# Hybrid decoder layer: small mixer steps later in TensorE's order, and w_out's block sums made from staged weights

## The chip, the cores and the metric

The kernel runs on one core of a Trainium2 chip. The metric is the device time of one execution in microseconds (us), as the median of several runs. The engines are named as in the profile: PE is TensorE (matmuls), DVE is VectorE, ACT is ScalarE, POOL is GpSimd and SP is SyncE, which here only issues DMAs. Each engine works through its own list of instructions in the order in which the program leaves it; between engines there are semaphores.

## The reference

One layer of a hybrid decoder, for a prompt of 2048 tokens and 8 x 4 decode tokens, 1024 channels, all in float32:

```python
proj = rms_norm(x, g_mix_norm) @ w_in          # 256 pool + 512 rnn + 512 gate branch + 256 query
o_pool = pool_mixer(...)                       # causal means over 2/4/8/16 tokens
xc = causal_dwconv(x_rnn, 4 taps)              # then two block-diagonal gates r and i
h  = rg_lru(xc, ...)                           # a = exp(c*r); h_t = a_t*h_(t-1) + sqrt(1-a_t^2)*i_t*xc_t
o_rnn = gelu(g_rnn) * h
o_xa = cross_attn(q, mk, mv)                   # 4 heads into 256 memory tokens
mix = concat(group_rms(o_pool), group_rms(o_rnn), group_rms(o_xa)) * g_mix_out
x = x + mix @ w_out
x = x + (gelu(dwconv(xn @ w_ff_gate)) * (xn @ w_ff_up)) @ w_ff_down
y = rms_norm(x, g_final)
```

It returns y, the new states of pooling, convolutions and recurrence, and the keys and values of the memory.

## The kernel before

Activations are kept with channels on the 128 partitions and tokens along the free axis. The tokens are cut in six column steps s = 0 to 5 of 344 or 348 columns, two to a block. A float32 operand of a matmul is split in a high and a low part (names h and l: ACT makes h by a copy, DVE makes l = x - h), and a product is three matmuls, hh, lh and hl.

Sweep 1 (up to about 250 us) is the recurrent mixer. For each step PE makes four projections: pr{s}0 and pr{s}1 (the recurrence's input) and pq{s}0 and pq{s}1 (the gelu branch), 48 matmuls each. Woven between them are PE's small steps: str (the sums of squares of the next step's x, one column per token tile), bcr (its reciprocal root broadcast over the partitions), sto and bco (the same for the mixer's output), and pg, four pairs of gate matmuls whose input is the convolved xc. Around them a loop runs through the other engines: DVE scales pr into xr and convolves it into xc (`L537`, six scalar_tensor_tensor at `L549` per half), PE makes pg, ACT r and i (`L471`), xc and r (`L482`, `L486`), a (`L488`) and a square root (`L490`), DVE i, the scan (`L491`, `L574`), g (`L591`), and then, in DVE's order, the squares of the next step (`L359`, `L349`), xr and the convolution of the next step. pr and pq share two PSUM buffers.

Where the small steps come in PE's order is set by the class Weave: each small step is a generator, each k step of a projection ticks a clock by its cost, and a generator is resumed once the clock has passed its due time. The due times are the table W.

```python
        yield 0.0, W["norm"] if s else W["norm_0"]
        yield from g_stat(l, 0, tj, J, rsx[:, s, :], name, W["stat"] if s else W["stat_0"])
```

Then come the memory's keys and values and sweep 2 (about 265 to 447 us): pooling, queries, cross-attention (pS scores, softmax on ACT and DVE, pT, pV), written to DRAM as mixp and mixr. Then w_out for block 0: eight outputs po00 to po07, each over eight k tiles of mix. The mix tiles (sm, split in ahm and alm) and the weight tiles (st_wo, split in h_wo and l_wo) go through one ring of three staging buffers, tag "stg":

```python
        st = wp.tile([P, 1024], F32, tag="stg", bufs=3, name="st_" + name)
```

The loads are issued by SP, whose order is that of the program and not a scheduler's; a load waits until the last reader of its buffer is done, and everything behind it on SP waits too. The other engines' order in the sweeps is set by a scheduler; behind them it is that of the program.

The rest (520 to 2120 us) multiplies blocks of 2 x 2 in seven products instead of eight. w_out for the other blocks comes first (the out stage). The class Pair loads four quarters wr11, wr12, wr21, wr22 of a weight pair, makes four sums s1 to s4 of them on DVE the first time (`L1036`), keeps s1 to s4 in DRAM for the following blocks, and makes the operands wt from them (`L1047`, `L1051`).

Of the kernel before, what the change touches and what calls it, by code (L numbers as in the profile page):

```python
# [43 lines left out]
def hybrid_kernel(ctx: ExitStack, tc: tile.TileContext, I, O):  # L44
# [12 lines left out]
    W = dict(pool_0=12.8, attn_0=1.42, soft0_0=9.0, st_p0=18.9, st_x5=13.5,  # L57
             norm_0=9.35, stat_0=2.55, prep_m=2.07, kv=11.0, gate=8.2, norm=14.0, stat=8.5, prep_r=9.7, mix_r=10.2,
             sq_r=1.6, st_r=22.5, mix_5=14.0, sq_5=1.4, st_5=7.0, bc_p=1.0, attn=0.42, soft0=8.5,
# [69 lines left out]

    def w_place(ring, shape, name, dtype):  # L130

        return wp.tile(shape, dtype, tag="w" + ring, bufs=8, name=name)

    def g_load_w(w, src, name, ring, parts=1):
        st = wp.tile([P, 1024], F32, tag="stg", bufs=3, name="st_" + name)
        w += [w_place(ring, [P, 1024], z + name, F32R) for z in ("h_", "l_")]
        for i in range(parts):
            c = slice(i * 1024 // parts, (i + 1) * 1024 // parts)
            nc.sync.dma_start(out=st[:, c], in_=src[:, c])
            split(w[0][:, c], w[1][:, c], st[:, c])  # L140
            yield
# [48 lines left out]
    xhl = [dr.tile([P, 2, 8, n], F32, name=f"xhl{s}") for s, n in enumerate(NCOL)]  # L190

# [172 lines left out]
    def g_norm(x, s, name):  # L364

        n = NCOL[s]
        tj, J = TOK[s]
        l = squares(x, n, name)
        yield 0.0, W["norm"] if s else W["norm_0"]
        yield from g_stat(l, 0, tj, J, rsx[:, s, :], name, W["stat"] if s else W["stat_0"])  # L370
        RB[s] = new_rb(name)
        yield from g_bcast(rsx[:, s, :], n, tj, J, RB[s][:, 0:n], name)
# [491 lines left out]
    wo = [load_w(I["w_out"][0], "wo00", "a")]  # L864
    mix = [load_mix(0, k, n) for k in range(KD)]
    wo += [load_w(I["w_out"][d], f"wo0{d}", "a") for d in range(1, 4)]
# [40 lines left out]
    def short(name, n):  # L907
# [6 lines left out]
          for nm, m in (("gate", 12), ("up", 12), ("down", 12), ("out", 4))}  # L914
# [82 lines left out]
    SEEN = set()  # L997

    class Pair:
# [7 lines left out]
        def load(self, first=False):  # L1007

            nm, q = self.nm, self.q
            self.a, self.sg, self.w = {}, {}, {}  # L1010
            for i, x in ((1, 2), (2, 1), (2, 2), (1, 1)) if first else ((2, 1), (2, 2), (1, 1), (1, 2)):
                if not self.make and (i, x) == (2, 1):
                    continue
                r = v4(f2.tile([P, 512], F32, tag="wr", bufs=NRAW, name=f"wr{i}{x}{self.name}"))
                if nm == "down":
                    g, j = q
                    z = I["w_down"][8 * g + 4 * x - 4:8 * g + 4 * x, :, 256 * j + 128 * i - 128:256 * j + 128 * i]
                    nc.sync.dma_start(out=r, in_=z.rearrange("k p c -> p k c"))
                else:
                    nc.sync.dma_start(out=r, in_=v4(I["w_" + nm][2 * q + i - 1][:, 512 * x - 512:512 * x]))  # L1020
                self.a[i, x] = r
# [19 lines left out]
        def form(self, i):  # L1041
            a, sg = self.a, self.sg
            return (a[1, 1], sg.get(2), sg.get(1), sg.get(3), a[2, 2], a[1, 2], sg.get(4))[i]
# [391 lines left out]

    def do(what, s):
        early.pop((what, s))()
# [15 lines left out]
    do("sigma1", 0)  # L1453
    B0.hi(2)
    B0.lo(2)
    for s in range(2):
        if s:
            do("sigma1", s)
        do("hi2", s)
        do("lo2", s)  # L1460
    for h in range(2):
        S.activation(out=y7[h], in_=y7[h], func=AF.Square)
        V.tensor_tensor(out=ssum["a0"][:, h], in0=ssum["a0"][:, h], in1=y7[h], op=ALU.add)
    for i in (1, 2, 3):
        for s in range(2):
            if i > 1:
                do(f"sigma{i}", s)
            if i < 3:
                do(f"keep{i}", s)
            if i == 2 and s == 0:  # L1470
                do("hi1", 0)
# [192 lines left out]
```

## Time and profile before

| | us |
|---|---|
| runs | 2121.68, 2122.81, 2124.09 (median 2122.81) |
| the profiled run, and its span | 2121.97, 2120.2 |
| PE busy | 2060.7 |
| DVE busy | 1612.6 |
| ACT busy | 1291.2 |
| POOL busy | 98.3 |

In the profile L12 is a line of the kernel, numbers of buffers are left out of names (po for po00 to po07), `out<-in` names what an instruction writes and reads, and x4 is the number of instructions in a row. PE is busy nearly everywhere, so the profile is read from PE's side: where it waits, what for, and what clock it was granted there.

### The profile page before, as it was taken

What the parts mean: (1) busy time and instruction counts of PE and PEld (TensorE: products, weight loads), DVE (VectorE), ACT (ScalarE), POOL (GpSimd) and SP (SyncE); (2) the same over time, 40 slices, a digit from 0 to 9 for tenths busy, and PEclk for the clock granted to TensorE, in tenths of its full rate; (3) what the DMA queues carried; (4) which work ended last, traced back from release to release, by engine and by line L of the source; (5) the groups of instructions that cost most, each with busy time, mean ns of one, the idle gap of its engine ahead of it and who ended that gap; (6) DMA issues with size and microseconds to landing.
All of it is one profiled execution on the core that took longest, in us unless ns stands there. A gap on an engine that the chain in (4) does not pass through costs nothing.

```text
span 2120.2 us, 35326 instructions
## 1 busy us (share of the span) xinstructions
PE 2060.7 (97%) x12996; PEld 2004.2 (95%) x12996; DVE 1612.6 (76%) x2801; ACT 1291.2 (61%) x2322; POOL 98.3 (5%) x136
## 2 busy tenths in 40 slices
PE   8999899999999999999999999999999999999997
PEld 7888798888899999999999999999999999999997
DVE  8777776874988888889897665668778665668774
ACT  7878834552656656566556665557666665557663
POOL 1111000000000000000000000000000000000001
PEclk9999999999999999999999999999999999999997
DMA  7233494335887656678996555677886554677882
GB/s 275 91 137 133 161 326 142 126 131 196 263 229 233 219 201 217 198 235 243 256 264 213 191 179 178 217 258 216 248 249 192 189 185 165 205 269 219 247 219 78
DMA packets 266892, 434.28 MB, mean 205 GB/s; under 512 B 25792, under 2 KB 124832, under 8 KB 266720
## 3 DMA queue, kind: packets, MB, share of 16 engines
q1 hardware_dynamic: 247248, 372.89, 53.4%
q0 software_dynamic: 18240, 57.63, 10.8%
q8 instruction: 102, 1.67, 0.3%
q10 hardware_dynamic: 1232, 1.51, 0.2%
q14 instruction: 70, 0.57, 0.1%
HBM read 297.69 MB, written 139.96 MB: 206 GB/s over the span
## 4 chain that ended last, share of the span: by engine, by line
PE 83%; DVE 5%; ACT 4%; DMA 4%; issue 3%; POOL 0%; SPq 0%; POOLq 0%; ACTq 0%; DVEq 0%
PE bg L1066 10%; PE bu L1066 10%; PE bd L1066 8%; PE ag L1066 6%; PE cg L1066 6%; PE cu L1066 6%; PE au L1066 6%; PE ad L1066 5%; PE cd L1066 5%; PE pq L234 4%; PE po L234 3%; PE bo L1066 2%; PE pu L234 1%; PE co L1066 1%; DMA wr11d<-in_w_down_dram 1%
## 5 line engine op out<-in xcount | busy, mean ns | idle before, releaser
L1164 DVE SCALAR_TENSOR_TENSOR cv<-gt,pv,cv 128x696 f32<-128x696 f32 (+2 forms) x144 | 133.0, 924 | 35.1 <-ACT cv L1159 35.1
L1180 DVE TENSOR_TENSOR u<-u,cv 128x696 f32<-128x696 f32 (+1 forms) x72 | 63.3, 879 | 62.5 <-ACT cv L1176 62.3
L1226 POOL DMA_DIRECT2D ys<-cd x32 | 34.8, 1121 | 1366.6 <-ACT cd L1095 1235.6
L1066 PE MATMUL bd<-h4s,wt4d 128*128 128x348 f32 (+1 forms) x288 | 72.9, 326 | 4.3 <-DVE cd L1088 4.3
L1066 PE MATMUL ag<-h5s,wt5g 128*128 128x348 f32 (+1 forms) x288 | 74.9, 323 | 0.0
L1066 PE MATMUL cg<-h6s,wt6g 128*128 128x348 f32 (+1 forms) x288 | 74.6, 322 | 0.0
L1066 PE MATMUL cg<-h2s,wt2g 128*128 128x348 f32 (+1 forms) x288 | 74.5, 322 | 0.0
L1066 PE MATMUL bg<-h1s,wt1g 128*128 128x348 f32 (+1 forms) x288 | 74.5, 321 | 0.0
L1066 PE MATMUL bg<-h3s,wt3g 128*128 128x348 f32 (+1 forms) x288 | 74.5, 321 | 0.0
L1066 PE MATMUL cu<-h6s,wt6u 128*128 128x348 f32 (+1 forms) x288 | 74.5, 322 | 0.0
L1066 PE MATMUL bg<-h4s,wt4g 128*128 128x348 f32 (+1 forms) x288 | 74.5, 321 | 0.0
L1066 PE MATMUL ag<-h0s,wt0g 128*128 128x348 f32 (+1 forms) x288 | 74.4, 321 | 0.0
L1066 PE MATMUL au<-h0s,wt0u 128*128 128x348 f32 (+1 forms) x288 | 74.4, 320 | 0.0
L1066 PE MATMUL bu<-h4s,wt4u 128*128 128x348 f32 (+1 forms) x288 | 74.4, 320 | 0.0
L1066 PE MATMUL bu<-h3s,wt3u 128*128 128x348 f32 (+1 forms) x288 | 74.4, 320 | 0.0
L1066 PE MATMUL bu<-h1s,wt1u 128*128 128x348 f32 (+1 forms) x288 | 74.4, 320 | 0.0
L1066 PE MATMUL au<-h5s,wt5u 128*128 128x348 f32 (+1 forms) x288 | 74.3, 321 | 0.0
L1066 PE MATMUL cu<-h2s,wt2u 128*128 128x348 f32 (+1 forms) x288 | 74.3, 321 | 0.0
L1066 PE MATMUL cd<-h6s,wt6d 128*128 128x348 f32 (+1 forms) x288 | 73.5, 327 | 0.0
L1066 PE MATMUL bd<-h3s,wt3d 128*128 128x348 f32 (+1 forms) x288 | 71.9, 321 | 1.6 <-ACT t6d L1084 1.6
L1066 PE MATMUL cd<-h2s,wt2d 128*128 128x348 f32 (+1 forms) x288 | 71.5, 321 | 0.0
L1066 PE MATMUL ad<-h5s,wt5d 128*128 128x348 f32 (+1 forms) x288 | 71.5, 321 | 0.0
(559 smaller groups left out, 7496.0 us busy)
## 6 DMA issues: line engine op xcount, KB each, us to landing
hs<-u SPq DMA_DIRECT2D x24, 696.0 KB, 4.1
ys<-cd POOLq DMA_DIRECT2D x20, 696.0 KB, 10.9
wr22g<-in_w_gate_dram SPq DMA_DIRECT2D x36, 256.0 KB, 4.3
wr11g<-in_w_gate_dram SPq DMA_DIRECT2D x36, 256.0 KB, 4.8
wr12g<-in_w_gate_dram SPq DMA_DIRECT2D x36, 256.0 KB, 5.1
wr22u<-in_w_up_dram SPq DMA_DIRECT2D x36, 256.0 KB, 6.6
wr11u<-in_w_up_dram SPq DMA_DIRECT2D x36, 256.0 KB, 6.5
wr12u<-in_w_up_dram SPq DMA_DIRECT2D x36, 256.0 KB, 6.5
```

Of the source, the lines that this page charges most:

```text
L234: T.matmul(o, w_[:, ks], z, start=(k == 0 and i == 0), stop=(k == nk - 1 and i == 2))
L1066: T.matmul(pt[:, 0:n], w[:, w_, ks_(k)], blk.hl[i][a_][:, k, :], start=(i in (0, 2) and k == m == 0), stop=(k == 3 and m == 2), skip_group ...
L1164: V.scalar_tensor_tensor(out=cv[:, z0:nn], in0=gt[:, z0 + t:nn + t], scalar=pcol("fcw", 3 * f + t), in1=cv[:, z0:nn], op0=ALU.mult, op1=AL ...
L1180: V.tensor_tensor(out=u, in0=u, in1=k["cv"][:, i, 0:nn], op=ALU.mult)
L1226: at[N + 14 + 1 + s].append(lambda j=2 * d + s, k=ks[s]: G.dma_start(out=flat(ys[b][j]), in_=qv(k["c"], n), accum_op=ALU.add, max_dma_last ...
```

## The change

There are two parts.

First, five due times of W become larger, and the first step's norm gets its own (norm_1, stat_1): gates 8.2 to 10.3, norm 14 to 20, st_x5 13.5 to 17, attn 0.42 to 2.5. Only sweep 1 changes in PE's order.

Second, four of w_out's blocks (wo00 to wo03) are loaded one after another ahead of the mix tiles. While their raw float32 is in the staging buffers, DVE makes the sums of the first two pairs from it (ws00 and ws01, ws10 and ws11, two sums in each) and POOL stores them to ws_out in DRAM. In the out stage these two pairs load the sums and two of the quarters instead of four quarters, and make and keep no sums.

```diff
-    W = dict(pool_0=12.8, attn_0=1.42, soft0_0=9.0, st_p0=18.9, st_x5=13.5,
-             norm_0=9.35, stat_0=2.55, prep_m=2.07, kv=11.0, gate=8.2, norm=14.0, stat=8.5, prep_r=9.7, mix_r=10.2,
-             sq_r=1.6, st_r=22.5, mix_5=14.0, sq_5=1.4, st_5=7.0, bc_p=1.0, attn=0.42, soft0=8.5,
+    W = dict(pool_0=12.8, attn_0=1.42, soft0_0=9.0, st_p0=18.9, st_x5=17.0,
+             norm_0=9.35, stat_0=2.55, norm_1=17.0, stat_1=4.5, prep_m=2.07, kv=11.0, gate=10.3, norm=20.0, stat=8.5, prep_r=9.7, mix_r=10.2,
+             sq_r=1.6, st_r=22.5, mix_5=14.0, sq_5=1.4, st_5=7.0, bc_p=1.0, attn=2.5, soft0=8.5,
...
-        st = wp.tile([P, 1024], F32, tag="stg", bufs=3, name="st_" + name)
+        st = STG[name] = wp.tile([P, 1024], F32, tag="stg", bufs=3, name="st_" + name)
...
+    ws_out = [dr.tile([P, 4, 512], F32, name=f"ws_out{q}") for q in range(4)]
...
-        yield 0.0, W["norm"] if s else W["norm_0"]
-        yield from g_stat(l, 0, tj, J, rsx[:, s, :], name, W["stat"] if s else W["stat_0"])
+        yield 0.0, W[f"norm_{s}" if s < 2 else "norm"]
+        yield from g_stat(l, 0, tj, J, rsx[:, s, :], name, W[f"stat_{s}" if s < 2 else "stat"])
...
-    wo = [load_w(I["w_out"][0], "wo00", "a")]
+    wo = []
+    for q in range(2):
+        wo += [load_w(I["w_out"][d], f"wo0{d}", "a") for d in (2 * q, 2 * q + 1)]
+
+        (a11, a12), (a21, a22) = ((z[:, 0:512], z[:, 512:1024]) for z in (STG.pop(f"wo0{2 * q + i}") for i in range(2)))
+        sa, sb = (tmp("t", [P, 2, 512], f"ws{q}{i}") for i in range(2))
+        V.tensor_tensor(out=sa[:, 0], in0=a21, in1=a22, op=ALU.add)
+        V.tensor_tensor(out=sa[:, 1], in0=sa[:, 0], in1=a11, op=ALU.subtract)
+        G.dma_start(out=ws_out[q][:, 0:2], in_=sa)
+        V.tensor_tensor(out=sb[:, 0], in0=a11, in1=a21, op=ALU.subtract)
+        V.tensor_tensor(out=sb[:, 1], in0=a12, in1=sa[:, 1], op=ALU.subtract)
+        G.dma_start(out=ws_out[q][:, 2:4], in_=sb)
     mix = [load_mix(0, k, n) for k in range(KD)]
-    wo += [load_w(I["w_out"][d], f"wo0{d}", "a") for d in range(1, 4)]
...
-    SEEN = set()
+    SEEN = {("out", 0), ("out", 1)}
...
-            for i, x in ((1, 2), (2, 1), (2, 2), (1, 1)) if first else ((2, 1), (2, 2), (1, 1), (1, 2)):
+            for i, x in ((1, 2), (2, 2)) if first else ((2, 1), (2, 2), (1, 1), (1, 2)):
...
+    v4(f2.tile([P, 512], F32, tag="sg", bufs=6, name="sg"))
...
     do("sigma1", 0)
+    do("sigma1", 1)
+    do("sigma2", 0)
+    do("sigma2", 1)
...
-    for i in (1, 2, 3):
-        for s in range(2):
-            if i > 1:
-                do(f"sigma{i}", s)
-            if i < 3:
-                do(f"keep{i}", s)
-            if i == 2 and s == 0:
-                do("hi1", 0)
```

How instructions move is shown at three places. The first is PE in sweep 1, at the start of step 3's pq (names with numbers: pq30 is step 3, half 0; h_wr4 and l_wr4 are the first weight tile of that half). Before:

```order
L234 MATMUL pr31_1475<-ahr33_1024,l_wr3_208 128x348
L164 MATMUL str4_1543<-ones_69,sqr4_1413 116x1 x3
L234 MATMUL pq30_1572<-ahr30_1018,h_wr4_223 128x348
L234 MATMUL pq30_1572<-alr30_1019,h_wr4_223 128x348
L234 MATMUL pq30_1572<-ahr30_1018,l_wr4_224 128x348
L468 MATMUL pg300_1576<-xc3_1406,bdg_123 128x348
L468 MATMUL pg301_1577<-xc3_1406,bdg_123 128x348
```

The statistic str4 stands ahead of pq30 and the first gate pair pg300, pg301 behind three of its matmuls. Now:

```order
L238 MATMUL pq30_1559<-ahr32_1026,l_wr4_228 128x348
L472 MATMUL pg300_1578<-xc3_1410,bdg_127 128x348
L472 MATMUL pg301_1579<-xc3_1410,bdg_127 128x348
L238 MATMUL pq30_1559<-ahr33_1028,h_wr4_227 128x348
L238 MATMUL pq30_1559<-alr33_1029,h_wr4_227 128x348
L238 MATMUL pq30_1559<-ahr33_1028,l_wr4_228 128x348
L238 MATMUL pq30_1559<-ahr33_1028,h_wr4_227 128x348
L238 MATMUL pq30_1559<-alr33_1029,h_wr4_227 128x348
L238 MATMUL pq30_1559<-ahr33_1028,l_wr4_228 128x348
L166 MATMUL sto2_1593<-ones_69,xc2_1034 116x1 x3
```

The first gate pair comes behind 18 matmuls of pq30, and str4 behind it and the second pair, after 30. The last gate pair moves too: it stood behind 3 or 6 matmuls of pq31 and stands behind 18, so 30 instead of 45 (step 2) or 42 matmuls of the step follow it.

The second is SP at w_out of block 0. Before:

```order
L139 DMA st_wo00_4565<-in_w_out_dram 128x1024
L299 DMA sm00_4571<-mixp0_78 128x688
L299 DMA sm01_4577<-mixp0_78 128x688
L299 DMA sm02_4583<-mixr0_75 128x688
L299 DMA sm03_4589<-mixr0_75 128x688
L299 DMA sm04_4595<-mixr0_75 128x688
L299 DMA sm05_4601<-mixr0_75 128x688
L299 DMA sm06_4607<-mixp0_78 128x688
L299 DMA sm07_4613<-mixp0_78 128x688
L139 DMA st_wo01_4619<-in_w_out_dram 128x1024
L139 DMA st_wo02_4625<-in_w_out_dram 128x1024
L139 DMA st_wo03_4631<-in_w_out_dram 128x1024
```

Now:

```order
L141 DMA st_wo00_4569<-in_w_out_dram 128x1024
L141 DMA st_wo01_4575<-in_w_out_dram 128x1024
L141 DMA st_wo02_4589<-in_w_out_dram 128x1024
L141 DMA st_wo03_4595<-in_w_out_dram 128x1024
L303 DMA sm00_4609<-mixp0_78 128x688
L303 DMA sm01_4615<-mixp0_78 128x688
L303 DMA sm02_4621<-mixr0_75 128x688
L303 DMA sm03_4627<-mixr0_75 128x688
L303 DMA sm04_4633<-mixr0_75 128x688
L303 DMA sm05_4639<-mixr0_75 128x688
L303 DMA sm06_4645<-mixp0_78 128x688
L303 DMA sm07_4651<-mixp0_78 128x688
```

Three weight tiles are moved ahead of the eight mix tiles. With the ring of three, st_wo03 waits for the sum ws01 that reads wo00 and wo01 (`L877` of the changed kernel), sm00 for the sum behind it (`L878`), sm01 for l_wo03, sm02 for alm00, sm03 for the last sum of ws11, sm04 for alm01, and so on.

The third is DVE at the same place, from the copy upo, the last of sweep 2's pooling. Before, alm07, l_wo01 and l_wo02 follow upo, and alm00 to alm06 stand ahead of it. Now:

```order
L858 COPY upo_4566<-qu5_4220 128x30
L874 TENSOR_TENSOR ws00_4581<-st_wo01_4575 128x512
L877 TENSOR_TENSOR ws01_4582<-st_wo00_4569,st_wo01_4575 128x512
L875 TENSOR_TENSOR ws00_4581<-ws00_4581,st_wo00_4569 128x512
L878 TENSOR_TENSOR ws01_4582<-st_wo00_4569,ws00_4581 128x512
L874 TENSOR_TENSOR ws10_4601<-st_wo03_4595 128x512
L877 TENSOR_TENSOR ws11_4602<-st_wo02_4589,st_wo03_4595 128x512
L123 TENSOR_TENSOR l_wo03_4597<-st_wo03_4595,h_wo03_4596 128x1024
L875 TENSOR_TENSOR ws10_4601<-ws10_4601,st_wo02_4589 128x512
L123 TENSOR_TENSOR alm00_4612<-sm00_4609,ahm00_4611 128x688
L878 TENSOR_TENSOR ws11_4602<-st_wo02_4589,ws10_4601 128x512
```

The eight sums come behind upo, and all of alm00 to alm07 behind the first seven of them. PE's order is the same at this place in both kernels: po00 reads ahm00 and alm00 first, then ahm01 and alm01, up to ahm07 and alm07.

More of the change, by code (lines that the diff above doesn't have):

```diff
@@ L128, in split_g @@
         V.scalar_tensor_tensor(out=lo, in0=src, scalar=g, in1=hi.bitcast(F32), op0=ALU.mult, op1=ALU.subtract)
+    STG = {}
     def w_place(ring, shape, name, dtype):
@@ L913, in hybrid_kernel @@
     WS = {nm: [dr.tile([P, 4, 512], F32, name=f"ws_{nm}{q}") for q in range(m)]
-          for nm, m in (("gate", 12), ("up", 12), ("down", 12), ("out", 4))}
+          for nm, m in (("gate", 12), ("up", 12), ("down", 12))}
+    WS["out"] = ws_out
     ssum = {}
@@ L1042, in form @@
             a, sg = self.a, self.sg
-            return (a[1, 1], sg.get(2), sg.get(1), sg.get(3), a[2, 2], a[1, 2], sg.get(4))[i]
+            return (a.get((1, 1)), sg.get(2), sg.get(1), sg.get(3), a[2, 2], a[1, 2], sg.get(4))[i]
         def hi(self, i):
@@ L1456, in hybrid_kernel @@
     for s in range(2):
-        if s:
-            do("sigma1", s)
         do("hi2", s)
         do("lo2", s)
+    for i in (3, 4):
+        for s in range(2):
+            do(f"sigma{i}", s)
+    do("hi1", 0)
     for h in range(2):
```

## The prediction

> **What bounds the kernel now.** I read the page first, then the waits of TensorE (PE) over the first 620 us, then stretches and the order of time at the places that the change touches.
>
> ```profile
> span 2120.2 us, 35326 instructions
> PE 2060.7 (97%) x12996; PEld 2004.2 (95%) x12996; DVE 1612.6 (76%) x2801; ACT 1291.2 (61%) x2322; POOL 98.3 (5%) x136
> PE 83%; DVE 5%; ACT 4%; DMA 4%; issue 3%; POOL 0%; SPq 0%; POOLq 0%; ACTq 0%; DVEq 0%
> ```
>
> PE is the bound: 97% busy, 83% of the chain. An edit pays only by taking idle time, or half-clock time, from PE. The idle time that this change can reach, as total, times and longest wait in us:
>
> ```profile
> PE str L164 <- DVE sqr L349: 8.8, 3, 5.3
> PE pg L468 <- DVE xc L549: 6.5, 3, 2.9
> ...
> PE pS L665 <- ACT e L641: 3.4, 1, 3.4
> ...
> PE bo L1066 <- ACT h1s L987: 1.5, 1, 1.5
> PE pq L234 <- DVE xr L537: 1.5, 1, 1.5
> PE bo L1066 <- DVE l1s L991: 1.2, 1, 1.2
> PE bo L1066 <- ACT t6o L1084: 1.0, 1, 1.0
> PE bo L1066 <- DVE wt1o L1051: 0.8, 1, 0.8
> ```
>
> str, pg and pq are sweep 1: 8.8 + 6.5 + 1.5 = 16.8 us. bo is the start of the out stage: 1.5 + 1.2 + 1.0 + 0.8 = 4.5. The clock beside the longer waits (stretch, its length, then busy times of PE, PEld, DVE, ACT and POOL; the next number is the granted clock):
>
> ```profile
> 148.00:158.00 10.00, 7.41 (x30) 5.37 (x30) 9.18 (x22) 4.71 (x7) 1.82 (x3) 0.66 0.22 86
> 230.00:240.00 10.00, 7.28 (x24) 5.17 (x25) 10.00 (x18) 6.45 (x10) 0.72 (x1) 0.66 0.45 145
> 446.00:455.00 9.00, 7.23 (x26) 4.75 (x26) 5.58 (x12) 4.01 (x12) 1.43 (x2) 0.62 0.96 366
> 538.00:544.00 6.00, 5.22 (x22) 4.98 (x23) 6.00 (x8) 6.00 (x11) 0.00 (x0) 0.72 0.92 279
> ```
>
> A clock of 0.66 over 10 us (1 is full, 0.5 half) is 6.8 us at half rate, so up to 3.4 us of work lost, about 2.5 where PE also stood idle. Three such places in sweep 1 make some 7 us.
>
> **Sweep 1: the small steps placed later.** The question is whether str and pg were placed too early, or their inputs come too late wherever they stand. I compare, from the end of a step's last gate matmul (pg) to the start of the next step's first, the time passed and PE's busy time in it (first and second number after the stretch):
>
> ```profile
> 44.64:74.07 29.43, 24.17 (x150) 23.53 (x150) 22.62 (x49) 25.17 (x35) 4.86 (x9) 0.90 0.38 146
> 86.49:110.45 23.96, 23.96 (x155) 23.72 (x154) 16.56 (x21) 21.61 (x30) 1.80 (x4) 1.00 0.25 98
> 123.00:151.91 28.91, 24.28 (x154) 23.74 (x155) 19.01 (x33) 25.28 (x33) 2.71 (x5) 0.97 0.35 124
> 167.11:191.67 24.56, 23.74 (x152) 23.24 (x151) 17.12 (x29) 22.73 (x32) 2.16 (x4) 1.00 0.30 102
> 204.60:232.72 28.12, 23.70 (x148) 23.12 (x148) 18.23 (x33) 24.94 (x35) 1.08 (x2) 0.99 0.43 143
> ```
>
> PE has about 24 us of work between the two; the rest is stall. In the new order the last pg moves back as far as the first pg of the next step: 30 + 96 + 18 matmuls stand between them where 45 + 96 + 3 stood, again 144, and str now comes behind the pg, which takes about half a us of cover away (23.4). So the loop gate, activations, scan, convolution, next gate gets no more cover. It only gains if ScalarE (ACT) and VectorE (DVE) do their part faster. That part, for the third row:
>
> ```profile
> 122.43 0.46 ACT L313 ACTIVATE rbr<-bcr 128x348 f32<-128x348 f32 x1
> ...
> 124.07 1.11 ACT L471 ACTIVATE r<-pg,gb 64x348 f32<-64x348 f32 x2
> ...
> 126.34 1.28 ACT L486 ACT_TABLE_LOAD   x1
> ...
> 129.36 1.80 ACT L486 ACTIVATE r<-r,sp 128x348 f32<-128x348 f32 x3
> 131.19 1.37 ACT L488 ACTIVATE a<-r 128x1392 f32<-128x1392 f32 x1
> ...
> 137.95 1.61 DVE L491 TENSOR_TENSOR i<-i,xc 128x1392 f32<-128x1392 f32 x1 [3.75 <-ACT xc L490]
> ...
> 147.21 0.88 DVE L537 TENSOR_TENSOR xr<-pr,rbr 128x696 f32<-128x696 f32 x1
> ...
> 149.22 3.04 DVE L549 SCALAR_TENSOR_TENSOR xc<-xr,pv,xc 128x348 f32<-128x348 f32 x6
> ```
>
> From the gate's end (123.00) to a it takes 8.2 us. In the new ACT order half of the r and xc pieces go between the gates and the extra table load is gone: 0.6 left over from the pair before, four pieces at 0.56, four at 0.6 and rbr at 0.46 make 5.7. From a to i (137.95) it is 6.8, and from i to the end of the fifth of the six taps (149.22 + 2.53) 13.8, as before: same operations, same order. The gate starts 0.1 behind that tap. Sum 26.4 against a cover of 23.4: a stall of 3.0 where 4.6 stood. The same sum for the others: into the second step 2.3 (before 0: there the table load and gelu now go ahead of the square root, 2.65 later), into the fourth 2.7 (before 0.8), into the fifth 3.0 (before 4.4). Into the first, the gates themselves start 12 matmuls or 1.9 us later, ACT has no idle time behind them to make that up, and xr's earlier place on DVE gives 0.8 back: about 5.5 (before 5.3). The pg that waits 1.65 in the last step keeps its distance: 1.9. Stalls 18.4 after, 16.8 before. Half-clock time shrinks, since the stalls are shorter and split in two (xr's buffer at pq, then pg): of 7 us some 2 to 7 stay. Together a gain of 3.6 to a loss of 1.6, unless the chains are mis-sized: 2 us in each of four would give 8 more. I take **3 us gained**, from 4 lost to 12 gained.
>
> The Trainium skill ("TensorE: Matmul & The Clock Gate", Part 1) has the clock fall only after an idle window of about 3.4 us, on a free-running count. By that, stalls of 3 us or less would keep it full, which is the 3.6. The trace disagrees as far as it goes: two waits of 2.70 and 1.93 us with work between them brought the 0.66 of 148 to 158.
>
> **Block 0's w_out: one load queue, three staging buffers.** This is the largest term. Before, the mix tiles sm are loaded while sweep 2 still runs:
>
> ```profile
> 385.56 14.92 SPq L299 DMA_DIRECT2D sm<-mixr  x4
> 412.85 14.13 SPq L299 DMA_DIRECT2D sm<-mixp  x2
> ...
> 431.82 0.56 PE L234 MATMUL po<-ahm,h_wo 128*128 128x344 f32 x2
> ...
> 440.27 0.18 DVE L854 COPY upo<-qu 128x30 f32<-128x30 f32 x1
> 440.37 0.87 DVE L123 TENSOR_TENSOR alm<-sm,ahm 128x688 fp32r<-128x688 f32 x1
> ...
> 441.71 0.47 PE L234 MATMUL po<-ahm,l_wo 128*128 128x344 f32 x2
> ...
> 445.75 1.06 ACT L122 ACTIVATE h_wo<-st_wo 128x1024 fp32r<-128x1024 f32 x1 [3.89 <-DMA st_wo<-in_w_out_dram]
> ```
>
> After, wo00 to wo03 stand ahead of all sm on SP, and a staging buffer is not free until the sums have read it. Three buffers hold wo00, wo01 and wo02; wo03 waits for the second sum; the eight sm are queued behind it. DVE reaches the sums right behind upo, so near 440, while PE's order is unchanged there and it stands at po00 at 431.8. Prices (groups of DVE and ACT by shape with busy us, then mean ns of one; and the loads of sm with their median us from issue to landing):
>
> ```profile
> L123 DVE TENSOR_TENSOR l_wo<-st_wo,h_wo 128x1024 fp32r<-128x1024 f32 x6 | 7.2, 1221 | 5.5 <-ACT h_wo L122 5.5
> L123 DVE TENSOR_TENSOR alm<-sm,ahm 128x688 fp32r<-128x688 f32 x8 | 7.0, 873 | 0.9 <-ACT ahm L122 0.6
> L122 ACT ACTIVATE ahm<-sm 128x688 fp32r<-128x688 f32 x8 | 6.2, 781 | 3.3 <-PE pu L234 2.2 <-DMA sm<-mixr 1.1
> L1036 DVE TENSOR_TENSOR s1o<-wr21o,wr22o 128x512 f32<-128x512 f32 x4 | 2.7, 682 | 0.0
> sm<-mixr SPq DMA_DIRECT2D x4, 344.0 KB, 3.5
> ```
>
> On before's clock: upo ends at 439.6 (the alm ahead of it is gone); two sums, 441.0; wo03 is issued and lands 4.5 later (as the third st_wo before: issued as alm ended at 441.2, split from 445.75), 445.5; two sums, 446.9; l_wo 448.1; a sum, 448.8; alm00 (its sm issued at 442.3, after the fourth sum) 449.6. PE's k = 0 starts 17.9 late. Behind it on PE stand the pS and pT of the softmax and every later po, and DVE's reductions of pS stand between alm00 and alm02, so PE's lateness comes back to DVE. Then three rounds through three buffers, each 3.5 + 0.78 + 0.87: sm01 goes out at 448.1, alm01 453.3; sm04 at 453.3, alm04 458.5; sm07 at 458.5, alm07 463.7; the others lie between. The last k ends at 464.8 against 442.2: 22.7 late. ACT has its softmax done meanwhile, so the wait of 3.4 at pS goes; the half-clock stretch moves with it. Net **19 us lost**; low end 14 (only the first delay counts: 17.9 - 3.4), high end 24 (a us more in each round, and the alm behind reductions of pS). wo01 and wo02, now split earlier, fall into idle time of ACT and DVE; without it 4 more splits would cost about 4 us.
>
> **The out stage.** Its first pair loses eight sums (8 x 0.60 of DVE) and eight keeping stores, and loads the sums that POOL stored. Of its waits 1.5 + 1.2 + 0.8 = 3.5 can go, and with them the half clock of 538 to 544 (0.72 of 6 us), another 1.7; t6o's 1.0 likely stays. Bounds 0 (h1s is late for another reason) and 6.2; I take **4.5 gained**, since DVE and the loads, for which PE waits there, are both relieved. POOL's four stores of sums lie on an engine that is 5% busy.
>
> **Sum.** The profiled run took 2121.97 us (span 2120.2), 0.8 under the median of 2122.81. 2122.81 - 3 + 19 - 4.5 = 2134.3; I say 2134.
>
> **Rivals.**
> - *Sweep 1 gives all it has.* All 16.8 of stall and 7 of half clock: 2122.8 - 24 + 19 - 4.5 = 2113, faster. For it: str's wait is the largest, and str does move behind work that is ready. Against: the equal 144 matmuls. Chance 0.11. With half of it, 2125: 0.17.
> - *The loads don't starve PE.* If sums and loads were done before 431.8: 2122.8 - 3 - 4.5 = 2115. Against: DVE's order and upo at 440. It would take PE itself being late there. 0.05.
> - *Starved harder.* Sweep 1 loses 4, po00 24, the out stage gives nothing: 2151. For it: every k now waits for its own load, at a falling clock. 0.07.
> - The forecast, 2127 to 2142: 0.60.
>
> **How the numbers follow.** A change of 0.2% (4.2 us) is what a measurement here tells from none. Below 2118.6: the first rival (0.11) and most of the second (0.03): 0.14. Between: half of sweep 1, 0.17, and the rest of the second, 0.02: 0.19. Above 2127: 0.67. The range runs from 2114, which leaves out the full gain of sweep 1 (0.11), to 2142, which leaves out the harder starvation (0.07).
>
> **What would show it.** PE idle near 432 to 450 with po waiting for ahm or alm, and st_wo issued as a ws sum ends: the large term. Stalls of 2 to 3 us at pg in the second to fifth steps, none at str: the loop. No wait at bo for h1s, l1s or wt1o: the out stage. I am wrong if sm loads land before 432, or if pg is reached without a wait in every step; both would make the kernel faster.

## The result, and the profile after

| | us |
|---|---|
| before, measured beside it | 2122.52 (2121.68 to 2124.09) |
| changed kernel | 2142.36 (2134.48 to 2147.06) |
| ratio | 1.0088, 95% interval 1.007 to 1.0106 |

The change costs 19.8 us. The sign is the predicted one. The time is 8 us above the predicted 2134 and 0.4 above the end of the range (2142). The four runs of the changed kernel lie far apart, with spans of 2145.2, 2138.1, 2132.7 and 2143.0 us at mean granted clocks of 0.977, 0.981, 0.983 and 0.978: span times clock is 2096 to 2098 in each, so the spans differ as the clock does. The profile is that of the slowest.

The head of its page, with the span and each engine's busy time:

```profile
span 2145.2 us, 35317 instructions
PE 2072.9 (97%) x12996; PEld 2015.6 (94%) x12996; DVE 1613.5 (75%) x2801; ACT 1290.5 (60%) x2322; POOL 100.7 (5%) x140
```

The number of PE's matmuls is the same, and PE is busy 12.2 us longer with them; the other 12.8 of the span's 25.0 us are idle time. PE's waits over the first 645 us (total, times, longest):

```profile
PE po L238 <- ACT ahm L122: 17.1, 2, 16.2
PE pq L238 <- DVE xr L541: 8.5, 4, 2.6
PE pg L472 <- DVE xc L553: 7.5, 3, 5.1
...
PE bo L1081 <- ACT t6o L1099: 2.9, 1, 2.9
PE bcx L316 <- DVE rsx L157: 2.6, 1, 2.6
...
PE sto L166 <- DVE xc L353: 1.1, 2, 0.8
```

Sweep 1 now waits 8.5 + 7.5 + 1.1 = 17.1 us where it waited 16.8. str is gone from the list, and pq's wait for xr stands in its place. The waits of 3.4 at pS and of 3.5 in all at bo for h1s, l1s and wt1o are gone; that for t6o has grown from 1.0 to 2.9. The new wait is po00's, 16.2 us for the high part of the first mix tile.

Where the time went is read from landmarks on PE, first those of before, then those of the changed kernel (the mem_kv product behind sweep 1, po00 to po07, the identity behind them, the statistics behind the out stage's first pairs; the two times in a row are the starts of the first and last):

```profile
L392 PE MATMUL pkv<-h_wkv,ahm x16: 389/394/484, 256.2 to 267.1; 128*128 128x512 f32 x16
L234 PE MATMUL pu<-ahp,l_wq x80: 314/322/327, 300.4 to 430.9; 128*128 128x348 f32 x64, 128*128 128x344 f32 x16
L1431 PE MATMUL bprime<-ident x12: 273/275/377, 520.1 to 522.0; 128*128 128x128 f32 x12
L164 PE MATMUL xsfa<-ones,ssa x40: 166/240/240, 551.3 to 891.5; 128*116 128x1 f32 x24, 128*86 128x1 f32 x16
```

```profile
L396 PE MATMUL pkv<-h_wkv,ahm x16: 389/394/484, 261.7 to 272.6; 128*128 128x512 f32 x16
L238 PE MATMUL pu<-ahp,l_wq x80: 315/322/327, 307.6 to 438.1; 128*128 128x348 f32 x64, 128*128 128x344 f32 x16
L238 PE MATMUL po<-ahm,h_wo x128: 313/321/656, 455.4 to 546.6; 128*128 128x344 f32 x128
L1446 PE MATMUL bprime<-ident x12: 272/275/377, 547.4 to 549.3; 128*128 128x128 f32 x12
L166 PE MATMUL xsfa<-ones,ssa x40: 166/240/240, 575.2 to 915.5; 128*116 128x1 f32 x24, 128*86 128x1 f32 x16
```

At the end of sweep 1 the changed kernel is 5.5 us late, at the last pu of sweep 2 7.2, at bprime 27.3, at xsfa 23.9, and 25.0 at the span's end. So in this profile sweep 1 loses 5.5, sweep 2's products 1.7, po00 to po07 20.1, the out stage gives back 3.4, and the rest loses 1.1.

Sweep 1 loses although its waits are as long as before. Up to mem_kv's first product PE is idle for 26.3 us before and 26.1 now, but busy for 229.9 and 235.6 us with the same matmuls. The granted clock (the third number from a row's end) tells why. This is the profile of before at its first wait, where the prediction showed the other two:

```profile
66.00:78.00 12.00, 7.08 (x32) 5.49 (x32) 12.00 (x26) 6.48 (x10) 2.20 (x5) 0.72 0.31 122
```

And these are the four stretches of the changed kernel's sweep 1:

```profile
70.00:90.00 20.00, 14.20 (x59) 10.88 (x59) 16.57 (x44) 10.25 (x16) 3.23 (x6) 0.66 0.24 95
150.00:162.00 12.00, 9.41 (x40) 8.15 (x38) 12.00 (x20) 5.72 (x8) 2.16 (x4) 0.72 0.32 128
230.00:242.00 12.00, 10.24 (x54) 9.34 (x52) 12.00 (x20) 8.33 (x12) 0.00 (x0) 0.86 0.15 46
253.00:262.00 9.00, 9.00 (x45) 7.76 (x43) 7.52 (x14) 6.95 (x12) 0.00 (x0) 0.81 0.38 123
```

With full and half as the only rates, 0.72 over 12 us is 2 x 0.28 x 12 = 6.7 us at half rate. Before, the three stretches make 6.7 + 6.8 + 6.8 = 20.3 us; after, the four make 13.6 + 6.7 + 3.4 + 3.4 = 27.1. That is up to 3.4 us more of lost work, and more of it lies where PE has work: in the last row PE is busy all 9 us at 0.81.

Around po00:

```profile
432.00:456.00 24.00, 7.82 (x61) 7.12 (x59) 17.06 (x51) 5.67 (x14) 1.81 (x4) 0.70 0.25 82
456.00:475.00 19.00, 17.58 (x80) 14.51 (x78) 10.85 (x20) 8.99 (x19) 1.65 (x3) 0.66 0.82 258
```

The wait itself is the first row (PE busy 7.82 of 24 us). The second is what comes behind it: PE is busy 17.58 of 19 us, at a clock of 0.66. What this second row costs is a question for the experiments.

Why the loads are late stands in the order of time. These rows are SP's issues (the second number is how long a group's issues stretch), then DVE's:

```profile
380.76 67.83 SPq L141 DMA_DIRECT2D st_wo<-in_w_out_dram  x4
449.55 5.77 SPq L303 DMA_DIRECT2D sm<-mixp  x2
```

```profile
393.42 1.21 DVE L123 TENSOR_TENSOR l_wo<-st_wo,h_wo 128x1024 fp32r<-128x1024 f32 x1
...
446.82 0.18 DVE L858 COPY upo<-qu 128x30 f32<-128x30 f32 x1
446.91 0.69 DVE L874 TENSOR_TENSOR ws<-st_wo 128x512 f32<-128x512 f32 x1
...
452.54 0.69 DVE L874 TENSOR_TENSOR ws<-st_wo 128x512 f32<-128x512 f32 x1 [3.01 <-DMA st_wo<-in_w_out_dram]
```

wo00 and wo01 are split by 394.6 (the first row is wo01's), so both are loaded, but the sums that read them come right behind upo, 52 us later. Until then three staging buffers are full, SP, which issued the first three st_wo by 382, sits at the fourth until 448, and the first sm is issued at 449.55.

### The profile page after: what moved, and what is told of

Read it like the earlier page. It is cut to its first block, busy times and chain, and to the rows that moved or that the text cites. A ratio compares the mean times of both kernels' runs of the same rounds, so it can differ in the third digit from the quotient of the medians.

```text
span 2145.2 us, 35317 instructions
## 1 busy us (share of the span) xinstructions
PE 2072.9 (97%) x12996; PEld 2015.6 (94%) x12996; DVE 1613.5 (75%) x2801; ACT 1290.5 (60%) x2322; POOL 100.7 (5%) x140
## 4 chain that ended last, share of the span: by engine, by line
PE 82%; DVE 6%; ACT 5%; DMA 3%; issue 3%; POOL 0%; SPq 0%; POOLq 0%; DVEq 0%; ACTq 0%
PE bg L1081 10%; PE bu L1081 10%; PE bd L1081 9%; PE ag L1081 6%; PE cg L1081 6%; PE cu L1081 6%; PE au L1081 6%; PE cd L1081 6%; PE ad L1081 6%; PE pq L238 4%; PE po L238 3%; PE bo L1081 2%; PE pu L238 1%; PE co L1081 1%; PE ao L1081 1%
## 5 line engine op out<-in xcount | busy, mean ns | idle before, releaser
L1241 POOL DMA_DIRECT2D ys<-cd x32 | 34.8, 1122 | 1367.8 <-ACT cd L1110 914.8
L238 PE MATMUL pq<-ahr,h_wr 128*128 128x348 f32 (+1 forms) x192 | 69.3, 361 | 9.2 <-DVE xr L541 8.5
```

The lines of the kernel that those rows point to most:

```text
L238: T.matmul(o, w_[:, ks], z, start=(k == 0 and i == 0), stop=(k == nk - 1 and i == 2))
L1241: at[N + 14 + 1 + s].append(lambda j=2 * d + s, k=ks[s]: G.dma_start(out=flat(ys[b][j]), in_=qv(k["c"], n), accum_op=ALU.add, max_dma_last ...
```

## The experiments

A ratio is to the kernel before, measured beside it on the same chip. The experiments ran on several chips, so two kernels with different befores are better compared by their ratios than by their times.

### Each part alone

`e1_order_only` is the kernel before with the new table W, norm_1 and stat_1, and nothing of w_out. `e2_sums_only` is the changed kernel with the old table.

> The kernel before with the new due times alone; w_out is loaded and summed as before. Theory A (the small steps moved, their inputs did not; the stalls stay and the clock falls for longer): the stalls of sweep 1 stay near 17 us, half-clock time there about 27 us instead of 20, the keys of the memory start 4 to 6 us later, total 2126 to 2130. Rival B (the order gains as it was meant to, and the whole loss is at w_out): at most 2119, with no wait at pg in the third to fifth steps.

> The changed kernel with the due times of before: only the loads and sums of w_out change. Theory A: PE waits 15 to 18 us ahead of po00, net of the wait at pS that goes some 18, and the out stage gives 3 to 4 back: 2134 to 2140. Rival B: all of the loss, so 2142 or more. Rival C (the wait at po00 is mostly taken from other waits): under 2130.

| | us | ratio, 95% interval |
|---|---|---|
| e1_order_only | 2126.02 | 1.0019 (1.0008 to 1.003) |
| e2_sums_only | 2134.6 | 1.0064 (1.0049 to 1.0079) |

The new order alone loses 3.0 us against the before beside it (2122.97), at the low end of what was expected of it, where the prediction had 3 gained. Its profile has the changed kernel's waits of sweep 1, to 0.1 us, and at the first of them its clock too:

```profile
PE pq L234 <- DVE xr L537: 8.5, 4, 2.6
PE pg L468 <- DVE xc L549: 7.5, 3, 5.1
...
PE sto L164 <- DVE xc L349: 1.1, 2, 0.8
```

```profile
70.00:90.00 20.00, 14.69 (x60) 11.36 (x60) 16.12 (x41) 10.02 (x15) 3.22 (x6) 0.66 0.24 95
```

The long first stretch belongs to the new order. It is 13.6 or 13.7 us of half clock in all five profiles whose sweep 1 is in the new order and otherwise untouched (the changed kernel, e1, e3, e5, e9), and 6.8 or 6.9 in the three in the old order (before, e2, e4). The rest varies: summed over windows of 4 us, all of sweep 1 has 23.8 to 24.0 us of half clock in the other four of the new order, and 27.1 only in the changed kernel's profile. mem_kv's first product starts at 256.2 to 258.3 us in the old order and at 259.2 to 261.7 in the new, 3.3 us later on average. So the order costs some 3 us, and the other 2 of the 5.5 in the profile after are that run's.

The sums alone lose 11.6, with the same wait at po00:

```profile
PE po L238 <- ACT ahm L122: 17.2, 2, 16.9
```

The two losses add up to 14.7, and the whole change loses 19.8; by the ratios 0.19% and 0.64% make 0.83% where the whole change has 0.88%. The intervals allow both that they add (12 to 23 us together against 15 to 22) and that they make each other worse; this stays open. Part of the difference between the two traces lies at bcx, behind the statistics stx among the po products, and has nothing to do with the change: from the last stx to bprime e2 takes 33.3 us and the changed kernel 35.9, around the same wait of 2.6 us, at clocks of 1.00 and 0.77 (the last section has more of these).

### The sums written in place

In `e3_sums_in_place` the sums go into the staging buffer that they were read from, not into two temporaries of the ring "t".

```diff
-        sa, sb = (tmp("t", [P, 2, 512], f"ws{q}{i}") for i in range(2))
-        V.tensor_tensor(out=sa[:, 0], in0=a21, in1=a22, op=ALU.add)
...
+        V.tensor_tensor(out=a22, in0=a21, in1=a22, op=ALU.add)
+        V.tensor_tensor(out=a21, in0=a11, in1=a21, op=ALU.subtract)
+        V.tensor_tensor(out=a11, in0=a22, in1=a11, op=ALU.subtract)
+        V.tensor_tensor(out=a12, in0=a12, in1=a11, op=ALU.subtract)
+        for i, z in enumerate((a22, a11, a21, a12)):
+            G.dma_start(out=ws_out[q][:, i], in_=z)
```

> The changed kernel, but the sums are written over the staged blocks instead of into the ring of temporaries, so that they need no buffer of the pooling's last step; loads, order of loads, due times and stores as in the change. Theory A (the sums stand behind the pooling because their output waits for its buffers, and the loads stand behind the sums): sums, wo03 and the mix tiles come some 40 us earlier, no wait at po00 over 4 us, total 2123 to 2130. Rival D (three more weight tiles ahead of the mix tiles in three staging buffers are enough to be late): PE still waits over 8 us at po00, total 2132 or more.

It took 2120.41 us, ratio 0.9987 (0.9976 to 0.9999), 22 us less than the changed kernel and 3 less than the lowest expected. SP's rows, and DVE's first sum:

```profile
379.17 20.41 SPq L141 DMA_DIRECT2D st_wo<-in_w_out_dram  x4
405.80 14.23 SPq L303 DMA_DIRECT2D sm<-mixp  x2
```

```profile
393.07 0.69 DVE L873 TENSOR_TENSOR st_wo<-st_wo 128x512 f32<-128x512 f32 x1
```

The first sum stands at 393 instead of 447, the four weight loads are issued within 20 us instead of 68, and the first sm 44 us earlier. Of po00's wait 1.4 us is left:

```profile
PE po L238 <- DVE alm L123: 1.4, 1, 1.4
```

So po00's starvation hangs on where the sums are written. Ring "t" has six buffers, which the mixers use until the last pooling is done; a sum that needs one of them comes in DVE's order behind that pooling. Loading the weights ahead of the mix tiles is not what cost 20 us: e3 does it too.

In `e4_pairs_in_place` the table is the old one, the sums are in place, and only the first pair of weights stays ahead of the mix loads; the second follows them.

> The due times of before; sums in place; only wo00 and wo01 ahead of the mix tiles, wo02 and wo03 behind them as before. Theory A: nothing left of either loss, the gain of the out stage stays: 2117 to 2121. Rival D: the staged pair holds the mix tiles back and PE waits at po00 by 3 us or more: 2122 to 2128.

2115.39 us, ratio 0.9966 (0.9955 to 0.9978): faster than both kernels, and 2 us below the lowest expected. Here the out stage's gain is seen without the losses:

```profile
L1448 PE MATMUL bprime<-ident x12: 273/275/377, 520.6 to 522.5; 128*128 128x128 f32 x12
L166 PE MATMUL xsfa<-ones,ssa x40: 166/240/241, 546.9 to 887.1; 128*116 128x1 f32 x24, 128*86 128x1 f32 x16
```

From bprime to xsfa it takes 26.3 us; before it took 31.2. It gains 4.9 against the 4.5 of the prediction, and its wait for t6o is 2.9, as in the changed kernel. This is the most of all the profiles: the ten kernels with these sums take 26.3 to 29.0 us there, 27.7 on average, and the four without them (before, e1, e6, e8) 30.8 to 32.1, on average 31.4. So the stage gains 3.7 us. The profile of e4 gains 2.3 us more behind xsfa, and where is not shown.

### The clock, with idle time filled

To tell the wait from the clock behind it, the next kernels issue matmuls of ident by ident into a PSUM tile that the following true product overwrites, so that PE is not idle while it waits.

```diff
+    def fill(z, m):
+        for _ in range(m):
+            T.matmul(z, ident, ident, start=True, stop=True)
...
         pt = psA(f"po0{d}")
+        if d == 0:
+            fill(pt[:, 0, 0:P], 110)
```

(e5_fill_po00 and, with 66, e9_fill_po00_66, on the changed kernel; in e6_fill_pg100 the line is `fill(pg[0][:, 0:P], 34 if (s, c) == (1, 0) else 0)`, on e1.)

> The changed kernel, and 110 matmuls of ident by ident (128x128, about 0.14 us each at the full clock, 15 us in all) into po00's PSUM tile ahead of its first true product; po00's first product overwrites them, so nothing that is computed changes. Theory A (the 16-us wait for the mix loads is lost twice: once as the wait, and again because TensorE, idle that long, is granted the half clock for the 27 us that follow): the wait for ahm falls to under 3 us, po00's first true product stands where it stood against pu's end (17 us behind it), the half-clock stretch at 441 to 469 us of the span shrinks from 27.3 to under 7, and the time falls by (27.3 - 7) / 2 = 10 us, to 2132 (2129 to 2135). Rival B (the half clock there does not come from the idle time): the stretch stays, and the time is 2140 to 2147. Rival C (DVE and the loads set the pace behind po00, not TensorE): the stretch goes and the time stays, 2139 to 2145.

> As e5_fill_po00, but with 66 of those matmuls: there each took 0.224 us at the full clock (24.7 us for 110), so that they ran 8 us past the arrival of the loads; 66 take 14.8 us and end inside the wait (17 us). Of the changed kernel's 27.3 us of half clock at 441 to 469 us, the part up to 455.4 lay in the wait and cost nothing; the 13.4 us behind it did 6.7 us of work at the full clock. Theory A (the clock behind the wait is a loss of its own): po00's first true product stands 17 to 18 us behind pu's end, the stretch is gone or under 4 us, and the time is 2142.4 less 6, 2136 (2134 to 2139). Rival C (DVE and the loads set the pace behind po00, not TensorE): the stretch goes, the waits behind po00 grow by as much, and the time is 2140 to 2144.

> The kernel before with the new table of numbers alone (e1_order_only), and 34 such matmuls (4.7 us) into pg100's tile ahead of its first product in step 1, where TensorE waits 5.06 us for xc. Theory A (what the table loses is the clock behind that one longer wait: half clock for 13.7 us where the kernel before has 6.8): the stretch at 73 us shrinks to under 3.4, mem_kv's first product comes 4 to 6 us earlier than 260.0, and the time is 2126.0 less 5, 2121 (2119 to 2123), level with the kernel before or just under. Rival B (sweep 1 is paced by DVE's loop, so that what TensorE gains in step 1 it waits for in step 2): the stretch goes, the waits for xr in steps 2 and 3 grow by as much, and the time stays 2124 to 2128.

| | us | ratio, 95% interval |
|---|---|---|
| e5_fill_po00 | 2143.34 | 1.0095 (1.007 to 1.012) |
| e9_fill_po00_66 | 2141.75 | 1.0088 (1.0073 to 1.0103) |
| e6_fill_pg100 | 2124.05 | 1.0001 (0.9992 to 1.0011) |

At po00 neither run shows what was expected. I had taken 0.14 us for one filler, but each is two matmuls in the trace, and together they take 0.22:

```profile
L248 PE MATMUL po<-ident 128*128 128x128 f32 x220 | 24.7, 275 | 0.0
```

110 of them ran past the loads, and po00 began 25.1 us behind pu's end (435.1 to 460.2) instead of 17.0. The clock stayed full up to 470 us, and of the 8.1 us that the fillers were too long, 5 came back by bprime (112.1 us from pu's end to it, against 109.0). In e9 the 66 fillers ended in the wait, 2.2 us of it were left, and the clock fell again, to 0.73 over 456 to 475 where the changed kernel has 0.66. From pu's end to bprime it took 108.7.

What a full clock behind po00 could give is read from the last mix tile that po00 needs. These are DVE's split of it (alm07) in the changed kernel and in e5:

```profile
472.01 0.87 DVE L123 TENSOR_TENSOR alm<-sm,ahm 128x688 fp32r<-128x688 f32 x1
```

```profile
468.07 0.88 DVE L123 TENSOR_TENSOR alm<-sm,ahm 128x688 fp32r<-128x688 f32 x1 [1.31 <-ACT ahm L122]
```

It is ready 34.4 us behind pu's end in the changed kernel, and 33.9 to 34.0 in e2, e5 and e9, although PE was granted 0.51 from 456 to 469 us in the first and the full clock in e5. In the changed kernel PE waits 0.4 us for it, and po01 starts 1.0 us behind it. So behind po00's first product the loads set the pace (rival C), and the half clock there costs about 1 us at most.

In sweep 1 the same means is clearer. e6's stretch:

```profile
70.00:90.00 20.00, 19.33 (x141) 17.02 (x141) 17.70 (x53) 12.46 (x21) 3.77 (x7) 1.00 0.38 131
```

The clock stays at 1.00 where e1 had 0.66. The fillers took 7.8 us in waits of 5.9, and yet mem_kv's first product came 3.0 us earlier (257.0 against 260.0). The waits for xr in the following steps stayed at 1.60, 2.58 and 2.59, so DVE's loop did not take the gain back. The time is level with the kernel before: 0.4 us over the before beside it, where e1 was 3.0 over. That is 2.6 us and not the 5 expected, and the overrun of 1.9 is most of what is missing. Not all of the gain is the filled stretch's: e6 has 6.9 us of half clock in the whole of sweep 1 and e1 has 24.0, so besides the filled 13.7 a stretch of 3.4 us is missing that the fillers did not touch.

`e7_pairs_filled` and `e10_pairs_filled_short` put fillers into six waits of e4, in e7 with numbers from the wrong price, in e10 from the measured one.

```diff
-        rms_stat([sq_list], one, tj, J, psC("st" + name), rs, name)
+        st = psC("st" + name)
+        fill(st[:, 0:P], {"r2": 21, "r4": 10}.get(name, 0))
+        rms_stat([sq_list], one, tj, J, st, rs, name)
...
         st = psC("bc" + name)
+        fill(st[:, 384:512], {"x5": 9}.get(name, 0))
...
             pg = [psC(f"pg{s}{c}{h}") for h in range(2)]
+            fill(pg[0][:, 0:P], {(3, 0): 7, (5, 0): 11, (5, 2): 6}.get((s, c), 0))
```

> The version with the sums in pairs and in place (e4_pairs_in_place, 2115.4), and such matmuls at its waits of 1.6 us and more in sweep 1 and at one of sweep 2: 34 ahead of str of step 1 (wait 5.24), 17 ahead of str of step 3 (2.67), 12 ahead of pg30 (1.93), 19 ahead of pg50 (2.92), 10 ahead of pg52 (1.64), 16 ahead of the last bcx (2.58). Theory A (the half clock follows the idle time and TensorE sets the pace): the stretches at 69, 151, 233 and 246 us, 20.4 us in all, go, mem_kv's first product comes up to 10 us earlier than 256.5, and the time is 2115.4 less 8, 2107 (2104 to 2111). Rival B (DVE's loop sets the pace of sweep 1): the stretches go, the waits grow by about as much, mem_kv's first product comes within 3 us of 256.5, and the time is 2112 to 2116.

> As e7_pairs_filled, with as many matmuls as fit into the waits at 0.224 us each: 21 ahead of str of step 1 (4.7 us in a wait of 5.24), 10 ahead of str of step 3 (2.2 in 2.67), 7 ahead of pg30 (1.6 in 1.93), 11 ahead of pg50 (2.5 in 2.92), 6 ahead of pg52 (1.3 in 1.64), 9 ahead of the last bcx (2.0 in 2.58). In e7 they ran 7.9 us past the waits, and mem_kv's first product came 5.2 us late: the clock gave back 2.7 only. Theory A (TensorE sets the pace, so that full clock behind the waits is gained): mem_kv's first product comes 3 us or more earlier than 256.5, and the time is 2115.4 less 3 to 8, 2110 (2107 to 2112.5). Rival B (DVE's loop takes back what the clock gives): mem_kv's first product within 2 us of 256.5, the time 2113 to 2117.

| | us | ratio, 95% interval |
|---|---|---|
| e7_pairs_filled | 2121.76 | 0.9994 (0.9983 to 1.0005) |
| e10_pairs_filled_short | 2110.9 | 0.9947 (0.993 to 0.9963) |

e7 lost 6 us to e4: its fillers ran 7.9 us past the waits. e10 is as expected, and its median is the lowest of all the kernels here; its interval still touches e4's (0.9955 to 0.9978). Its profile is that of its fastest run (2106.95 us). Sweep 1 of e4, then of e10, with mem_kv's first product in each:

```profile
50.00:262.00 212.00, 195.28 (x1156) 176.61 (x1156) 164.25 (x350) 173.56 (x251) 21.31 (x38) 0.95 0.37 130
...
L396 PE MATMUL pkv<-h_wkv,ahm x16: 389/394/484, 256.5 to 267.4; 128*128 128x512 f32 x16
```

```profile
50.00:262.00 212.00, 207.42 (x1294) 189.45 (x1293) 166.41 (x360) 177.28 (x254) 21.31 (x38) 1.00 0.40 143
...
L403 PE MATMUL pkv<-h_wkv,ahm x16: 389/394/484, 250.6 to 261.6; 128*128 128x512 f32 x16
```

The waits for DVE are still there, since the fillers lie in them. The clock goes from 0.95 to 1.00, and mem_kv comes 5.9 us earlier. With the 55 fillers of sweep 1 taken off (13.0 us) PE is busy 7.1 us less up to that product than in e4. In sweep 1 the half clock behind the waits is thus worth some 6 us in these two profiles; by their ratios the two kernels lie 4 us apart.

### DVE's part of the loop

`e8_no_gate_mult` is e1 without the product g = g * xc at the end of a mixer step. The product of gelu and h is left out, so its time is that of a smaller computation.

> The kernel before with the new table of numbers alone (e1_order_only), less DVE's product of g and xc at each mixer step's end (L591, 1.60 us each, six of them); the mixers' first output is then gelu's alone, and what follows is computed from that. Theory A (the waits of sweep 1 are DVE's loop: the conv of a step stands behind the last step's scans and this product, and the table only moves the wait from one place to another): the waits for xr and pg in steps 2 to 5 (2.2, 2.6, 2.6 and 3.8 us) each fall by about 1.6 us, 5 to 6.5 in all, and with the clock that they cost the time is 2126 less 6 to 9, 2119 (2116 to 2121). Rival B (the waits are set by the chain through ACT and TensorE, not by DVE's load): they fall by under 0.5 us each and the time is 2124 to 2127.

```profile
PE pg L468 <- DVE xc L549: 7.8, 5, 3.6
...
PE sto L164 <- DVE xc L349: 2.2, 3, 1.5
PE pq L234 <- DVE xr L537: 0.6, 1, 0.6
```

2116.32 us, ratio 0.9973 (0.9959 to 0.9987). The waits of sweep 1 make 7.8 + 2.2 + 0.6 = 10.6 us where e1 has 17.1. In steps 2 to 5 they fell from 11.2 to 5.3, four times 1.5, and one product takes 1.60; mem_kv came at 254.7, 5.3 us earlier than in e1. So these waits are DVE's part of the loop, which the table moves to other places (17.1 us for 16.8) and does not shorten.

`e11_pairs_late_mult` is e4 with this product moved into the first small step behind the mixer step, and `e12_pairs_late_mult_filled` adds fillers to that.

```diff
-        V.tensor_tensor(out=g, in0=g, in1=xc, op=ALU.mult)
...
         tj, J = TOK[s]
+        if nch == 4:
+            V.tensor_tensor(out=o, in0=o, in1=sqn, op=ALU.mult)
         S.activation(out=sqn, in_=o, func=AF.Square)
```

> The version with the sums in pairs and in place (e4_pairs_in_place, 2115.4), with DVE's product of g and xc moved from the end of a mixer step into the first small step behind it (it stands behind the next step's first xr on DVE then, ahead of its conv). All of the reference is computed. Theory A (the waits of sweep 1 are DVE's loop, and xr's part of it is shortened by the product's 1.60 us): the wait for xr in step 5 (1.50) goes, those for pg (1.93, 2.92, 1.64), which also stand behind the conv, stay within 0.7, mem_kv's first product comes 2 to 4 us earlier than 256.5, and the time is 2113 (2110 to 2115). Rival B (the product, moved, pushes the conv and g's mix back by its own length): the waits for pg grow by about 1 us each and the time is 2116 to 2120.

> The late product of e11_pairs_late_mult and matmuls into its waits as in e10_pairs_filled_short, their numbers cut to what e11's waits hold at 0.224 us each: 16 ahead of str of step 1 (3.6 us in a wait of 4.07), 9 ahead of str of step 3 (2.0 in 2.35), 4 ahead of pg30 (0.9 in 1.13), 9 ahead of pg50 (2.0 in 2.46), 4 ahead of pg52 (0.9 in 1.23), 9 ahead of the last bcx (2.0 in 2.58), and 8 ahead of the first bcr (1.8 in 2.97). Theory A (the two gains add up: e11 took 1.4 us of wait from sweep 1's first str and 0.8 from pg30, e10 took the half clock): mem_kv's first product at 248 to 249.5 (e10: 250.65), and the time 2109 (2106.5 to 2110.5), below e10's 2110.9. Rival B (in e10 the full clock already leaves DVE's loop as the pace, or the shorter waits come out in other places): level with e10, 2110.5 to 2113.

| | us | ratio, 95% interval |
|---|---|---|
| e11_pairs_late_mult | 2113.49 | 0.9958 (0.9942 to 0.9973) |
| e12_pairs_late_mult_filled | 2115.46 | 0.9965 (0.9952 to 0.9979) |

In e11 step 5's wait for xr went, the waits for pg fell by 0.4 to 0.8, and mem_kv came 3.5 us earlier (253.0). That is the expected size, but the interval overlaps e4's. e12 missed: the two gains don't add up. A wait that e11 hardly has (0.7) stands in its step 5:

```profile
PE sto L166 <- DVE xc L362: 4.6, 1, 4.6
```

```profile
235.72 0.87 DVE L551 TENSOR_TENSOR xr<-pr,rbr 128x696 f32<-128x696 f32 x1
236.51 0.87 DVE L362 TENSOR_TENSOR xc<-xc 128x696 f32<-128x696 f32 x1
237.30 1.21 DVE L123 TENSOR_TENSOR l_wkv<-st_wkv,h_wkv 128x1024 fp32r<-128x1024 f32 x1
238.44 0.51 DVE L362 TENSOR_TENSOR xc<-xc 128x348 f32<-128x348 f32 x1
```

The two folds that sto waits for have xr and a weight split ahead of and between them here; in e11 both folds are done before xr. That order is the scheduler's, and the fillers changed it.

## Why the prediction was right or wrong

**Sweep 1: wrong, "3 us gained".** The half that argued with the loop held. Stalls of 18.4 us were forecast and 17.1 came; into the first step 5.1 + 0.8 (forecast 5.5), the second 1.6 + 0.6 (2.3), the third 2.6 (3.0), the fourth 2.6 (2.7), the last step's pg 1.8 (1.9). Only the fifth is off, 1.8 for 3.0. e8 shows that the waits follow DVE's work.

What failed is the sentence "Half-clock time shrinks, since the stalls are shorter and split in two": 0 to 5 of the 7 us of work that the half clock cost were to come back. Instead half-clock time went from 20.3 us to 27.1 in the changed kernel and to some 24 in the other profiles with the new order. The first step's wait, 5.3 us at str before and 5.1 at pg after, has 13.6 us of half clock around it instead of 6.7; another wait of 0.8, at sto, follows it closely, but that this is the reason is not shown. e6 takes this stretch away, and with it most of the table's loss.

The 3 us were optimistic by the prediction's own sum too: 5 of clock less 1.6 of stalls is a gain of 3.4 (it says 3.6), the other end was a loss of 1.6, and the 3 leaned on a further 8 that chains wrong in size might give. The term measures 3.0 lost in e1's median, 3.3 in the mean of the profiles and 5.5 in the changed kernel's: the first two lie inside its bound of 4 lost, the last beyond it.

**po00: right in mechanism, 20.1 for 19, which is partly luck.** DVE reached the sums at 446.9; 440 on before's clock plus the 7.2 by which PE was late makes 447.2. po00's first product was forecast 17.9 late, and came 17.0 behind pu's end where it stood 0.6 behind it before: 16.4. The last k tile of po00 was forecast 22.7 late and was 24.4, net of sweep 2's 7.2, and the loads set its pace as forecast. More than the 3.4 of pS came back behind it: by stx the lateness was 24.8, 17.6 net. The bcx wait of 2.6, which is in both kernels, then added a stretch of half clock that the profile of before lacks, and 2.6 us of lateness. So the loads' own part is 17.6, and it is this stretch, which e2 and e4 lack too, that brings it to 20.1. What the prediction took as given, that the sums have to stand behind upo, is itself an effect of the temporaries: e3 shows it.

**The out stage: right, 3.7 for 4.5.** It is 3.4 in the changed kernel, 4.9 in e4 and 3.7 in the mean of the profiles. The waits for h1s, l1s and wt1o went, but for 0.2 us of two of them in e3. t6o's did not stay at 1.0 but rose to 2.9, and that wait is now the stage's only one; in the changed kernel a stretch of half clock lies beside it (0.94 over 547 to 576, 3.5 us).

**The sum.** Against the profile: sweep 1 was off by 8.5, sweep 2's products by 1.7, po00 by 1.1, the out stage by 1.1, and the rest by 1.1, 13.5 us, all to the same side; the profiled run lies 4.7 us above its median, so against the median it is 8. Some 5 of the 13.5 are this run's clock, 2 in sweep 1 and 2.6 at bcx.

**The rivals.** That sweep 1 gives its 16.8 us fell by the equal cover, as argued. That the loads don't starve PE was given 0.05 and was wrong for this kernel, but it needs only another place for the sums (e3). Of the harder starvation, sweep 1's part came near (5.5 in the profile and 3.3 in the mean, where it took 4); po00 stayed at 20.1 where it took 24, and the out stage did give its gain.

**The clock.** In the changed kernel the clock falls beside waits of 2.6 us (150 to 162 us: 0.72) and of 1.8 (253 to 262: 0.81), and the stretches of half clock are 3.4, 6.7 and 13.6 us long. The prediction set the Trainium skill ("TensorE: Matmul & The Clock Gate", Part 1) against the row at 148 to 158 us. The runs go on disagreeing that an idle time of about 3.4 us is needed. With its window of that length they agree: the lengths are near multiples of it.

## What to carry to other kernels

A staging buffer is only free once its last reader has run, and a reader can be late for the place it writes to: before extra readers are put on a buffer that an in-order load queue depends on, look which ring their outputs come from. A wait on the bounding engine has two prices, its length and the granted clock behind it, and they don't move together; a change that only moves waits can lose by the second. Where a load queue sets the pace, as behind po00, the second is hardly paid. Matmuls that fill a wait are worth trying where nothing shortens it, but only if their number comes from a measured duration: 108 in place of 64 turned a gain of 4.5 us into a loss of 6.

## What was not expected of the hardware

The same wait with the same work around it brings the half clock in one run and not in the other. At bcx PE waits 2.6 us in the changed kernel and in e4. The 15 us around it in the one and in the other:

```profile
510.00:525.00 15.00, 12.42 (x67) 12.36 (x67) 3.65 (x15) 0.46 (x1) 1.98 (x3) 0.77 1.01 356
```

```profile
486.00:501.00 15.00, 12.41 (x84) 12.36 (x83) 6.29 (x18) 1.57 (x3) 1.99 (x3) 1.00 1.01 351
```

PE's busy time is the same, but it did 67 matmuls in one and 84 in the other, and the clock is 0.77 and 1.00. What it costs is read from the last stx to bprime, in which PE has the same work in all the kernels. In eleven profiles with this wait of 2.6 us it takes 33.3 us in four (before, e2, e4, e6; clock full), 34.8 or 34.9 in two (e3, e5) and 35.9 or 36.0 in five (the changed kernel, e1, e8, e9, e11). Before, e1 and e8 are one and the same kernel at this place. So a wait of this length has a price of 0, 1.5 or 2.6 us that its length does not tell. That would fit four runs of one kernel lying 12.6 us apart at different mean clocks, though their single stretches were not compared. And the stretch outlasts its cause by more than I took it to: 13.6 us of half clock around a wait of 5.1, in all five profiles of that order.
